# RMSNorm on one core: the first load on 14 DMA engines instead of 16

## The chip, the core and the metric

The kernel runs on one core of a Trainium2 chip. The metric is the device time of one execution in microseconds (us), the median of several runs. A core has five engines with instruction streams of their own: TensorE (PE), VectorE (DVE), ScalarE (ACT), GpSimd (POOL) and SyncE (SP). Sixteen DMA engines move data between HBM, where input and output lie, and SBUF, the memory of 128 partitions in which the engines compute.

## The reference

```python
def reference(x, gamma):            # x: 16 x 1024 x 512 float32, gamma: 512 float32
    eps = 1e-5
    rms = np.sqrt(np.mean(x ** 2, axis=-1, keepdims=True) + eps)
    return (x / rms * gamma).astype(np.float32)
```

Each of the 16,384 rows of 512 numbers is divided by its root mean square and multiplied by gamma. 33.55 MB are read and as much is written.

## The kernel before, in words

The rows are cut into four tiles t = 0 to 3. In a tile each of the 128 partitions holds R = 32 rows that lie one after another in HBM, so a partition's part of a tile is one run of 64 KB. Three SBUF buffers of a whole tile, `slots[0]` to `slots[2]`, hold the tiles; tile 3 uses slot 0 again. A row is overwritten in place by its result.

All DMAs are issued by SyncE, in an order written out by hand. `load(t, slot, r0, r1)` (line 44) brings rows r0 to r1 of all 128 partitions of tile t; `store` (line 48) sends them out. Ahead of any computing SyncE issues, in this order: row 0 of tile 0 ("the first transfer", 256 KB, 2 KB for each partition), rows 1 to 8 ("the second transfer", 14 KB for each partition), gamma in five pieces with the bounds 0, 128, 224, 320, 416, 512 into `gamma_row`, rows 8 to 16, rows 16 to 32, and rows 0 to 16 of tile 1. The scheduler gives DMAs eight semaphores in turn; a DMA whose semaphore was used eight DMAs earlier waits until that one has landed. So the load of rows 16 to 32, the ninth DMA, waits for the first transfer, and the load of tile 1, the tenth, for the second.

TensorE multiplies a row of ones with `gamma_row` (line 66), which puts gamma on all 128 partitions of PSUM (`gamma_psum`); ScalarE copies it to `gamma_b` (line 166) for GpSimd, which works from SBUF.

The rows are then worked on in nine groups (line 76): of 7 and 9 rows of tile 0 first, then of 16 rows. For a group `square_sums` (line 89) squares its rows on ScalarE (line 96) and sums them on VectorE (line 97); `inverse_rms` takes the root on ScalarE (line 102) and the reciprocal on VectorE (line 103). The last rows of a group (`share`, 3 to 7 of them) are scaled and multiplied by gamma on GpSimd (lines 109, 110); the others are scaled on ScalarE, row by row (line 118), and multiplied by gamma on VectorE (line 122). The squares of the group ahead are taken before the scaling of the present one. After each group `transfers` (line 129) issues its stores and further loads:

```python
if (t, g) == (0, 0):
    load(1, 1, 16, 32)
    store(0, 0, 0, 1)
    load(2, 2, 0, 23)
elif (t, g) == (0, 7):
    store(0, 0, 1, 16)
```

The first group needs rows 0 to 7, so the first Square of ScalarE waits for the first two transfers.

Of the kernel before, what the change touches and what calls it, by code (L numbers as in the profile page):

```python
# [9 lines left out]
def kernel(  # L10
# [6 lines left out]
    nc = tc.nc  # L17
    P = nc.NUM_PARTITIONS
# [7 lines left out]
    N, D = xf.shape  # L26
# [3 lines left out]
    xv = xf.rearrange("(t p r) d -> t p r d", p=P, r=R)  # L30
# [9 lines left out]
    slots = [const.tile([P, R, D], fp32, name=f"slot{i}") for i in range(3)]  # L40

    before_scale = []

    def load(t, slot, r0, r1):
        dma = nc.sync.dma_start(out=slots[slot][:, r0:r1], in_=xv[t][:, r0:r1])  # L45
        before_scale.append((slot, r0, r1, dma))

    def store(t, slot, r0, r1):
# [1 line left out]
        before_scale.append((slot, r0, r1, dma))  # L50

    gamma_row = const.tile([1, D], fp32)
    pieces = (0, 128, 224, 320, 416, D)

    load(0, 0, 0, 1)
    load(0, 0, 1, 8)
    for c0, c1 in zip(pieces, pieces[1:]):
        nc.sync.dma_start(out=gamma_row[:, c0:c1], in_=gamma.unsqueeze(0)[:, c0:c1])
    load(0, 0, 8, 16)
    load(0, 0, 16, 32)  # L60
    load(1, 1, 0, 16)
# [105 lines left out]
    for k, group in enumerate(groups):  # L167
        t, g, n, pieces, share = group
# [45 lines left out]
```

## Time and profile before

| | |
|---|---|
| median of 3 runs | 161.56 us (161.54 to 161.67) |
| the profiled execution | 161.71 us, its span 159.9 us |
| busy | DVE 112.0, ACT 107.8, POOL 106.4, PE 2.0 us |
| DMA | 67.12 MB, mean 420 GB/s over the span |
| the first transfer | issued at 0.74 us |
| first Square of ScalarE | starts at 8.33 us |
| last store | issued at 139.2 us |

The span reaches from the first to the last instruction of the program; what the execution counts beyond it lies around the program. A page gives the busy time of each engine, 40 equal slices of the span with the busy share of each engine in tenths, the DMA queues, and the chain of work that ended last. The queue q1 carries the kernel's own transfers, q14 the fetching of instructions. In a row of the timeline there stand the start, the time, the engine (SPq is SyncE's queue), the line, the operation with what it writes and reads, and in brackets how long the engine was idle before and what ended that. A row of the windows has the stretch and its length, the busy times of PE, weight loads, DVE, ACT and POOL with the number of instructions, the clock granted to TensorE, the mean busy share of the 16 DMA engines, and GB/s.

### The profile page before, as it was taken

What the parts mean: (1) busy time and instruction counts of PE and PEld (TensorE: products, weight loads), DVE (VectorE), ACT (ScalarE), POOL (GpSimd) and SP (SyncE); (2) the same over time, 40 slices, a digit from 0 to 9 for tenths busy, and PEclk for the clock granted to TensorE, in tenths of its full rate; (3) what the DMA queues carried; (4) which work ended last, traced back from release to release, by engine and by line L of the source; (5) the groups of instructions that cost most, each with busy time, mean ns of one, the idle gap of its engine ahead of it and who ended that gap; (6) DMA issues with size and microseconds to landing.
All of it is one profiled execution on the core that took longest, in us unless ns stands there. A gap on an engine that the chain in (4) does not pass through costs nothing.

```text
span 159.9 us, 275 instructions
## 1 busy us (share of the span) xinstructions
PE 2.0 (1%) x2; PEld 0.5 (0%) x2; DVE 112.0 (70%) x39; ACT 107.8 (67%) x108; POOL 106.4 (67%) x24
## 2 busy tenths in 40 slices
PE   0050000000000000000000000000000000000000
PEld 0010000000000000000000000000000000000000
DVE  0019098899798999999999999999999009800000
ACT  3071967976999999999889999989960990000000
POOL 1000951994999599999999999999999990000000
DMA  5999999999998999998999999996996996999993
GB/s 182 431 430 467 451 402 434 467 410 393 385 554 389 377 453 407 434 467 381 420 453 443 410 459 451 516 476 286 508 500 279 525 508 279 426 484 402 402 500 148
DMA packets 2603, 67.12 MB, mean 420 GB/s; under 512 B 297, under 2 KB 298, under 8 KB 682
## 3 DMA queue, kind: packets, MB, share of 16 engines
q1 hardware_dynamic: 2602, 67.11, 98.0%
q14 instruction: 1, 0.01, 0.0%
HBM read 33.56 MB, written 33.55 MB: 420 GB/s over the span
## 4 chain that ended last, share of the span: by engine, by line
DVE 59%; ACT 22%; DMA 4%; ACTq 0%; issue 0%; SPq 0%
DVE ss L97 36%; DVE slot L122 23%; ACT slot L118 8%; ACT slot L96 7%; ACT sq_psum L96 6%; DMA slot<-in_x_dram 4%; DVE ss L103 1%; ACT ss L102 1%; ACTq L209 0%; ACT gamma_b L166 0%; SPq L45 0%; ACTq L96 0%
## 5 line engine op out<-in xcount | busy, mean ns | idle before, releaser
L109 POOL TENSOR_TENSOR slot<-slot,ss 128x3584 f32<-128x3584 f32 (+2 forms) x9 | 46.9, 5215 | 24.2 <-DVE ss L103 24.2
L110 POOL TENSOR_TENSOR slot<-slot,gamma_b 128x3584 f32<-128x3584 f32 (+2 forms) x9 | 59.2, 6583 | 0.7
L97 DVE TENSOR_REDUCE ss<-sq_psum 128x7 f32<-128x3584 f32 (+1 forms) x13 | 42.2, 3247 | 13.7 <-ACT sq_psum L96 13.7
L118 ACT ACTIVATE slot<-slot,ss 128x512 f32<-128x512 f32 x75 | 47.2, 707 | 4.7 <-DVE ss L103 4.7
L122 DVE TENSOR_TENSOR slot<-slot,gamma_psum 128x4608 f32<-128x4608 f32 (+2 forms) x9 | 41.3, 4590 | 8.7 <-ACT slot L118 8.7
L96 ACT ACTIVATE sq_psum<-slot 128x3584 f32<-128x3584 f32 (+1 forms) x13 | 34.5, 2656 | 6.3 <-DMA slot<-in_x_dram 5.7
L97 DVE TENSOR_REDUCE ss<-slot 128x9 f32<-128x4608 f32 x3 | 14.9, 4953 | 4.4 <-ACT slot L96 4.2
L97 DVE TENSOR_REDUCE ss<-sq_sbuf 128x5 f32<-128x2560 f32 x5 | 14.0, 2802 | 0.0
L96 ACT ACTIVATE slot<-slot 128x4608 f32<-128x4608 f32 x3 | 12.1, 4032 | 0.0
L96 ACT ACTIVATE sq_sbuf<-slot 128x2560 f32<-128x2560 f32 x5 | 11.6, 2323 | 0.5 <-DMA slot<-in_x_dram 0.5
L102 ACT ACTIVATE ss<-ss,eps_t 128x16 f32<-128x16 f32 (+2 forms) x9 | 2.7, 304 | 11.5 <-DVE ss L97 11.5
L103 DVE RECIPROCAL ss<-ss 128x16 f32<-128x16 f32 (+2 forms) x9 | 2.1, 235 | 0.4 <-ACT ss L102 0.4
L66 PE MATMUL gamma_psum<-gamma_row,ones_col 1*128 1x512 f32 x2 | 2.0, 1122 | 8.8 <-DMA gamma_row<-in_gamma_dram 8.8
L72 ACT ACT_TABLE_LOAD x1 | 1.3, 1283 | 1.2 <-PEq L198 1.2
L166 ACT COPY gamma_b<-gamma_psum 128x512 f32<-128x512 f32 x1 | 0.6, 566 | 0.0
L66 PEld LDWEIGHTS gamma_psum<-gamma_row,ones_col 1*128 1x128 f32 x2 | 0.5, 305 | 8.8 <-issue 8.8
L64 POOL MEMSET ones_col<- 1x128 f32 x1 | 0.2, 194 | 0.3 <-POOLq L198 0.3
L198 POOL MEMSET const-float32-0.0<- 128x1 f32 x1 | 0.1, 99 | 0.2 <-issue 0.2
L72 ACT ACTIVATE table<-eps_t 128x1 f32<-128x1 f32 x1 | 0.2, 203 | 0.0
L198 POOL MEMSET const-bfloat16-1.0<- 128x1 bf16 x1 | 0.1, 102 | 0.0
L198 POOL MEMSET const-uint8-127<- 128x1 uint8 x1 | 0.1, 102 | 0.0
L198 POOL MEMSET const-float32-1.0<- 128x1 f32 x1 | 0.1, 99 | 0.0
(1 smaller groups left out, 0.1 us busy)
## 6 DMA issues: line engine op xcount, KB each, us to landing
slot<-in_x_dram SPq DMA_DIRECT2D x5, 4096.0 KB, 24.3
out_dram<-slot SPq DMA_DIRECT2D x3, 4096.0 KB
out_dram<-slot SPq DMA_DIRECT2D x1, 7936.0 KB
slot<-in_x_dram SPq DMA_DIRECT2D x1, 5888.0 KB
out_dram<-slot SPq DMA_DIRECT2D x1, 3840.0 KB
slot<-in_x_dram SPq DMA_DIRECT2D x1, 2304.0 KB, 25.9
slot<-in_x_dram SPq DMA_DIRECT2D x1, 2048.0 KB, 10.0
slot<-in_x_dram SPq DMA_DIRECT2D x1, 1792.0 KB, 7.1
```

The lines of the kernel that those rows point to most:

```text
L66: nc.tensor.matmul(gamma_psum[:, 0], ones_col, gamma_row, start=True, stop=True)
L72: nc.scalar.activation(out=table, in_=eps_t, func=AF.Sqrt)
L96: nc.scalar.activation(out=sq[:, :m], in_=rows, func=AF.Square)
L97: nc.vector.tensor_reduce(out=ss[:, r : r + m, 0], in_=sq[:, :m], axis=mybir.AxisListType.X, op=OP.add)
L102: nc.scalar.activation(out=ss[:, :n, 0], in_=ss[:, :n, 0], func=AF.Sqrt, bias=eps_t, scale=1.0 / D)
L103: nc.vector.reciprocal(out=ss[:, :n, 0], in_=ss[:, :n, 0])
L109: nc.gpsimd.tensor_tensor(out=part, in0=part, in1=by_row, op=OP.mult)
L110: last = nc.gpsimd.tensor_tensor(out=part, in0=part, in1=gamma_b.to_broadcast([P, share, D]), op=OP.mult)
L118: nc.scalar.activation(out=x[:, g + r, :], in_=x[:, g + r, :], func=AF.Copy, scale=rstd[:, r])
L122: scaled = nc.vector.tensor_tensor(out=part, in0=part, in1=gamma_psum.to_broadcast([P, r1 - r0, D]), op=OP.mult)
L166: nc.scalar.copy(out=gamma_b[:, 0], in_=gamma_psum[:, 0])
L198: nc = _bacc.Bacc("TRN2", target_bir_lowering=False, num_devices=1)
```

## The change

The first transfer takes row 0 of 126 partitions only. Row 0 of the last two partitions follows as a DMA of its own behind the second transfer. Gamma comes in four pieces of 128 numbers where there were five, so that seven DMAs still stand ahead of the load of rows 8 to 16. By the description of the change the first transfer then runs on 14 of the 16 DMA engines. The instructions of the other engines and their order stay as they were.

```diff
-    def load(t, slot, r0, r1):
-        dma = nc.sync.dma_start(out=slots[slot][:, r0:r1], in_=xv[t][:, r0:r1])
+    def load(t, slot, r0, r1, p0=0, p1=P):
+        dma = nc.sync.dma_start(out=slots[slot][p0:p1, r0:r1], in_=xv[t][p0:p1, r0:r1])
         before_scale.append((slot, r0, r1, dma))
...
-    pieces = (0, 128, 224, 320, 416, D)
-
-    load(0, 0, 0, 1)
+    pieces = (0, 128, 256, 384, D)
+    wide = P - 2
+
+    load(0, 0, 0, 1, 0, wide)
     load(0, 0, 1, 8)
+    load(0, 0, 0, 1, wide, P)
     for c0, c1 in zip(pieces, pieces[1:]):
         nc.sync.dma_start(out=gamma_row[:, c0:c1], in_=gamma.unsqueeze(0)[:, c0:c1])
     load(0, 0, 8, 16)
```

## The prediction

> **What bounds the kernel now.** I read the page first: its 40 slices, then the queue table.
>
> ```profile
> span 159.9 us, 275 instructions
> DMA  5999999999998999998999999996996996999993
> q1 hardware_dynamic: 2602, 67.11, 98.0%
> q14 instruction: 1, 0.01, 0.0%
> ```
>
> The 16 DMA engines are busy for 98.0% of the span, while no compute engine passes 70% in the page's first part. A kernel like this ends when its slowest DMA engine has moved its share, so I looked at the DMA by stretches, and at what the DMA queue waits for.
>
> ```profile
> 1.70:3.70 2.00, 0.00 (x0) 0.00 (x0) 0.00 (x0) 0.95 (x2) 0.00 (x0) 1.00 1.05 336
> 3.70:8.30 4.60, 0.00 (x0) 0.00 (x0) 0.00 (x0) 0.00 (x0) 0.00 (x0) 1.00 1.00 419
> 57.00:100.00 43.00, 0.00 (x0) 0.00 (x0) 43.00 (x16) 40.74 (x43) 42.76 (x7) 1.00 1.01 433
> 100.00:140.00 40.00, 0.00 (x0) 0.00 (x0) 31.02 (x11) 26.01 (x33) 31.57 (x6) 1.00 1.00 432
> 140.00:158.00 18.00, 0.00 (x0) 0.00 (x0) 0.00 (x0) 0.00 (x0) 0.00 (x0) 1.00 0.99 426
> ```
>
> The last two figures are the DMA share and GB/s. Share 1.00 in every stretch: the engines are never short of work, even in the last 18 us when nothing computes. The start (336 and 419 GB/s) is poorer than the plateau (432).
>
> ```profile
> 0.74 0.86 SPq L45 DMA_DIRECT2D slot<-in_x_dram  x2
> 1.65 1.48 SPq L58 DMA_DIRECT2D gamma_row<-in_gamma_dram  x5
> 3.17 5.89 SPq L45 DMA_DIRECT2D slot<-in_x_dram  x4
> 8.33 3.16 ACT L96 ACTIVATE sq_psum<-slot 128x3584 f32<-128x3584 f32 x1 [5.67 <-DMA slot<-in_x_dram]
> 8.81 1.19 PE L66 MATMUL gamma_psum<-gamma_row,ones_col 1*128 1x512 f32 x1 [8.81 <-DMA gamma_row<-in_gamma_dram]
> ```
>
> This timeline of the start shows the seven issues that the change touches, and the two instructions that wait for their data.
>
> Last, the trace's single packets. A packet's record has start, duration and size, not its engine; but in steady work a packet starts 4 ns before its engine's previous one ends, so from 7.2 us on the records chain into 16 engines. The last packets of the 16 end between 157.96 and 158.63 us, at a mean of 158.19. Two engines stand apart: one ends at 158.62 ("the last"), one at 158.39; the next are 158.31 and 158.24. The last packet's mark on its semaphore comes at 159.03, SyncE ends its wait at 159.05, the span ends at 159.92, and the execution counts 161.71 us. From the last packet on everything is a fixed tail of 3.09 us, so the time moves one for one with the latest engine. The median of the three runs, 161.56, is 0.15 below this execution; I add differences to the median.
>
> Where the late ones lose time: one engine also carries the instruction packet, 8 KB, from 1.77 to 2.69 us; its first row packet starts at 2.72, against 1.75 to 2.38 on the others. The last engine lost its time in the second transfer: three of its packets there took 0.62, 0.74 and 0.79 us where 0.535 is usual, about 0.54 us in all. In that transfer the 16 engines lost a mean of 0.25 us to such stalls. (Chains in this ramp are less certain.)
>
> **The change part by part.** *First transfer.* 126 rows on 14 engines are nine 2 KB packets each where eight were; such packets follow each other at 80 ns, so 14 engines get +0.08 us. The other two engines lose eight packets, 0.64 us. They can begin the second transfer when its descriptors arrive: it is issued 0.44 us after the first (1.18 and 0.74), and the first one's packets start 1.01 us after their issue, so at about 2.19; that transfer began on the engines at 2.61 to 3.36. So a relieved engine is ahead by 0.4 to 0.9 us, and by 0.64 if it is the one with the instruction packet, where it starts at 2.70.
>
> *The issue of 126 rows.* No row shows one. Bounds: 0.23 us (the shortest one-row issue) and 0.43 us (the longest 128-row one), against 0.38; so -0.15 to +0.05 us on the start of every engine. I take 0, as the row count is nearest to the 128-row issues.
>
> *The two left rows.* 80 ns on each of two engines or 160 ns on one, and about 10 ns for each semaphore packet, behind the second transfer. They land after their engine's second-transfer packets; ScalarE's first Square at 8.33 waits for the last of those (landed 8.24), so it moves by 0 to +0.2 us. That is covered: the first store that needs the result is issued at 27.37, and the engines reach it at about 41.7.
>
> *Gamma.* A 512 B piece with its semaphore packet holds its engine for 29 ns, a 384 B one for 25: five took 0.128 us, four take 0.116, a gain of 0.012 on one engine. That engine ended at 158.23; with two more rows and the gain it ends at 158.38, below 158.62 still.
>
> *SyncE's queue.* Five issues (0.33, 0.23, 0.25, 0.25, 0.25 us) stand between the second transfer and the load of rows 8 to 16; the two-row issue takes the place of one, -0.1 to +0.2 us. Behind it that load is issued at 3.17; the engines reach it at 7.24 at the earliest, so 4 us cover it. The next loads wait for the landings of the first and second transfers (3.72, 8.26) and start on the engines at 12.1 and 21.8. The matmul waits for gamma until 8.81, and its result is first read at 15.65. If the cover at the first load were gone, 0.2 us would go straight to the end. There are still seven DMAs ahead of that load, so the waits of later DMAs on earlier ones keep their places.
>
> *A rule about the small transfer.* The row: the first transfer took from 0.74 to 3.71 to land, 3.0 us for 256 KB, yet five tiny gamma transfers behind the second one landed 0.19 us apart and held their engine for 0.13 us in all. The Trainium skill (DMA: Bandwidth & Descriptors, "Rules for kernel authors") says that under 64 KB a transfer is mostly overhead, and speaks of a fixed cost of about 2 us each. If that were paid in engine time, the new 4 KB transfer would make 163.5; the gamma packets speak against it, the latency lies beside other packets.
>
> *Sum.* If the last engine is one of the two relieved, the end passes to the next: 158.39 + 0.08 = 158.47, -0.15 us; if both late ones are, 158.31 + 0.08 = 158.39, -0.23. Forecast -0.16: 161.40, inside what a measurement of this kernel can tell from no change (0.2%, 0.32 us).
>
> **The rivals.** *The last engine is not one of the two.* It then does nine rows: +0.08 us, 161.64; if the transfer is spread otherwise than the change says, 161.56. For it: the records name no engine, and two of 16 is not many. Against: just two engines stand apart, and lateness from an instruction packet belongs to a fixed place.
>
> *A second hint on place.* The Trainium skill (same page, "Latency and other measured facts") says that engines 7 and 15 are usually slower than the rest, with a guess at a cause. This trace shows equal speed in steady work (1.213 us for 927 of the 1024 packets of 32 KB) and lateness only from the start, so the rule isn't borne out here as a rate; by it, engine 15 relieved would be the forecast, engine 7 late the rival above.
>
> *Slower: a start stall on an engine with nine rows.* The 0.54 us stall of the second transfer falls on another engine, as two engines now read that transfer while 14 still read the first. On an average engine 158.19 + 0.08 + 0.54 = 158.81, +0.19 us, 161.75; on the late one 158.39 + 0.08 + 0.54 = 159.01, +0.39, 161.95. It decides once any engine is over 0.43 us behind the mean. For it: that stretch stalled several engines by 0.1 to 0.5 us. Against: two engines ahead spread the crowd.
>
> *A larger gain.* The start stalls shrink for all. If all engines ended at their mean, 158.19 + 0.08 = 158.27, -0.35 us, 161.21; without the mean stall of 0.25 also, -0.60, 160.96. For it: the start moves 336 and 419 GB/s against 432. Against: 14 of 16 still start together.
>
> **How the numbers follow.** Forecast 0.36, larger gain 0.22, last engine not relieved 0.17, slower 0.25. Range: 161.00 to 161.95, which holds all but the ends of the outer two. Faster by over 0.2% (under 161.24): the larger gain and 0.11 of the forecast, should the first issue be also shorter, 0.33. Slower by over 0.2% (over 161.88): two thirds of the slower rival, 0.17, and 0.04 for a longer first issue with an unrelieved last engine, 0.21. Within: 0.46.
>
> **What would show it.** Right: nine packets of 2 KB on 14 engines, two engines whose first packets are of 14 KB near 2.2 to 2.7 us, last packets ending at 158.4 to 158.5, and a DMA share of 1.00 to the end. Wrong: a last engine at 158.7 or later with a stalled second transfer; a first packet later than 1.75 (the issue); or a DMA share under 0.95 after 57 us, which would mean that the engines wait for compute.

## The result and the profile after

The changed kernel took 162.12 us (median of 18 executions, 161.61 to 163.82) where the kernel before took 161.60 beside it: ratio 1.0049, 95% interval 1.0029 to 1.0070 (close to the ratio of the two means, 1.0048; the two medians alone give 1.0032). That is slower, by more than the 0.2% bound, and outside the range that was given. Of the single times half lie between 161.6 and 162.0, the other half between 162.2 and 163.8, and the median falls in the gap between the two halves. So in this measurement the change costs some 0.2 us in every execution and a half to two more in half of them. The kernel before has such long executions too, but fewer: two of its 18 (162.25 and 163.10 us). The profiled execution of the changed kernel is a long one, 163.11 us with a span of 161.3 (before: 161.71 and 159.9), and shows where these go.

The page and, under it, the DMA by stretches (last two figures: mean busy share of the 16 engines, GB/s):

```profile
span 161.3 us, 274 instructions
...
DMA  5999999999998999999999999899699799699990
...
q1 hardware_dynamic: 2600, 67.11, 97.2%
```

```profile
1.70:3.70 2.00, 0.00 (x0) 0.00 (x0) 0.00 (x0) 0.94 (x2) 0.00 (x0) 1.00 1.05 341
3.70:8.30 4.60, 0.00 (x0) 0.00 (x0) 0.00 (x0) 0.00 (x0) 0.00 (x0) 1.00 1.00 413
140.00:158.00 18.00, 0.00 (x0) 0.00 (x0) 0.00 (x0) 0.00 (x0) 0.00 (x0) 1.00 0.99 430
158.00:160.20 2.20, 0.00 (x0) 0.00 (x0) 0.00 (x0) 0.00 (x0) 0.00 (x0) 1.00 0.04 15
```

Up to 158 us hardly anything is lost: the engines are busy, and 430 GB/s in the last stretch is no less than the 426 before. The loss is a tail. The last of the 40 slices is empty but for little, and from 158.0 to 160.2 the share is 0.04 where the same stretch of before has 0.00:

```profile
158.00:160.20 2.20, 0.00 (x0) 0.00 (x0) 0.00 (x0) 0.00 (x0) 0.00 (x0) 1.00 0.00 0
```

So one engine works alone at the end. (Packets are counted where they start; the last packet starts before 158.9.) Chaining the single packets as in the prediction gives it: 15 engines move their last packet by 158.04 to 158.43 us, the sixteenth by 160.11, 1.67 us later. Before, the last one was 0.24 behind the next.

That engine can be followed back. It is the one that carries the instruction packet, here from 2.32 to 2.69 us. Its rows of the first transfer then take 2.68 to 3.70: nine packets in 1.02 us instead of 0.72, single ones of 0.09 to 0.22 us where 0.084 is usual, at a time when the others already move 14 KB packets. Behind the second transfer, at 8.12, it moves one of the two left rows; the other left row lies on the engine of gamma, at 7.43, just ahead of the four gamma pieces. So one of the two left rows fell on the engine that was already late. The Trainium skill (DMA: Bandwidth & Descriptors, "Why a DMA increments its semaphore by 16 and not by 1") says that a transfer that can't use all 16 engines uses the lowest-numbered ones; that the left row lies on the engine of gamma, whose transfers have one engine, agrees with it. By that rule a short first transfer can only ever relieve the highest-numbered engines; no trace here numbers the engines.

The start in the timeline:

```profile
0.74 1.19 SPq L45 DMA_DIRECT2D slot<-in_x_dram  x3
1.97 1.13 SPq L60 DMA_DIRECT2D gamma_row<-in_gamma_dram  x4
3.14 6.30 SPq L45 DMA_DIRECT2D slot<-in_x_dram  x4
8.96 3.16 ACT L98 ACTIVATE sq_psum<-slot 128x3584 f32<-128x3584 f32 x1 [6.31 <-DMA slot<-in_x_dram]
```

The issues stand as foreseen (the load of rows 8 to 16 at 3.14, before 3.17). The first Square starts at 8.96, 0.63 us later than before, as it waits for the late engine. That isn't what makes the tail: the last store is issued at 140.0 us (139.2 before), and the engines reach it at 148.4 at the earliest.

The late engine then falls back further, in steps. Its lag behind the next one, at the end of each load, in us, worked out from the packets:

| end of load, about | before | changed |
|---|---|---|
| tile 0, rows 8 to 16 (13 us) | 0.14 | 0.46 |
| tile 1, rows 0 to 16 (32 us) | 0.14 | 0.51 |
| tile 1, rows 16 to 32 (42 us) | 0.22 | 0.65 |
| tile 2, rows 0 to 23 (57 us) | 0.20 | 1.14 |
| tile 3, rows 0 to 16 (91 us) | 0.26 | 1.29 |
| tile 3, rows 16 to 32 (101 us) | 0.24 | 1.76 |
| last store (158 us) | 0.24 | 1.67 |

The four jumps, from 42 us on, are the four loads that a store follows. In the last three, the late engine's packets that lost most began at 55.71, 89.33 and 99.81 us (0.39, 0.16 and 0.47 us over the usual), and each was in work while the other 15 turned to stores (56.4 to 56.7, 90.3 to 90.6, 100.6 to 101.0 us). In the loads that end at 91 and 101 us these two packets are the only ones of any engine that took over 0.08 us more than usual; before the change no packet did. In the loads that end at 42 and 57 us packets of all engines lose time, in both kernels. Where another load follows (13 to 32 us, and the short load of tile 2 that ends at 82 us) and in the stores, the lag changes by less than 0.1 us.

### The profile page after: what moved, and what is told of

Same layout as the page of the kernel before. It is cut to its first block, busy times and chain, and to the rows that moved or that the text cites. A ratio compares the mean times of both kernels' runs of the same rounds, so it can differ in the third digit from the quotient of the medians.

```text
span 161.3 us, 274 instructions
## 1 busy us (share of the span) xinstructions
PE 2.0 (1%) x2; PEld 0.5 (0%) x2; DVE 112.1 (70%) x39; ACT 107.8 (67%) x108; POOL 106.4 (66%) x24
## 4 chain that ended last, share of the span: by engine, by line
DVE 36%; ACT 28%; DMA 21%; SPq 1%; ACTq 0%; issue 0%
DMA slot<-in_x_dram 21%; DVE ss L99 19%; DVE slot L124 17%; ACT slot L120 11%; ACT slot L98 7%; ACT sq_psum L98 7%; ACT sq_sbuf L98 1%; ACT ss L104 1%; SPq L45 0%; ACTq L211 0%; DVE ss L105 0%; ACT gamma_b L168 0%; SPq L49 0%; ACTq L98 0%
```

## The experiments

The theory I wanted to test ("L") says two things: the lag of one engine at the start makes the time, and it grows where the others have turned from loads to stores. Rivals: a small transfer behind the second one costs by itself ("N"); rows spread otherwise than eight to an engine make packets collide ("P"). The kernels were timed in three groups, each on one chip and with the kernel before beside it: first the even splits, 8 KB and 16 KB; then 2 KB, the work for all engines alike, the late lag and the run without a first transfer; then 4 KB, the left rows on one engine, 120 partitions and the changed kernel once more. In the three groups 4 of 23, 4 of 35 and 2 of 35 executions of the kernel before took over 162.2 us.

**Even splits.** Rows split so that every engine has eight row packets in all.

```diff
-    wide = P - 2
+    wide = 64
```

> The first transfer takes 64 partitions (four rows on each engine if all 16 are used), the other 64 follow behind the second transfer; gamma in four pieces. The work is even over the engines, as before the change. Theory L (one engine, the one that also carries the instruction packet, is pushed behind the others at the start, and its lag grows whenever the others have turned from loads to stores while it still loads): no engine gets more rows, so the lag at the start of the load of rows 8 to 16 stays at 0.1 to 0.3 us, and the time at 161.5 to 161.8. Theory N (a small row transfer behind the second one costs by itself, by its issue or its place in the queue): slower as the changed kernel, 161.8 to 163.5. Theory P (a spread of rows over the engines other than that of 128 partitions makes small packets collide with the 14 KB packets): some cost, 161.7 to 162.5, if 64 partitions are spread otherwise.

Measured: 162.22 us, ratio 1.0045 (1.0022 to 1.0068). The 161.5 to 161.8 that I had by L was wrong, and the time alone would fit N and P. But the kernel is slower by another way than N's: the trace has no late engine (lag 0.22 us at 13 us, 0.05 at the end). All 16 are late alike: they begin the load of rows 8 to 16 at a mean of 8.05 us instead of 7.51. With four rows fewer ahead of it the second transfer began earlier (14 KB packets from 2.54 us on), but its first packets took 0.53 to 1.55 us, most over 0.88, and most ended at 3.5 to 4.1 us, so the rows moved behind it were added work and nothing was won in front.

```diff
-    wide = P - 2
+    wide = 112
```

> The first transfer takes 112 partitions (seven rows on each of 16 engines), the other 16 partitions follow behind the second transfer, one row on each engine; gamma in four pieces. Even work, but seven rows for each engine, so the rows lie on other partitions of an engine than with 128. Theory L: as before the change, 161.5 to 161.8, lag 0.1 to 0.3 us. Theory P: row packets of 100 to 220 ns in the place of 84 once other engines read 14 KB packets, first large packets of over 0.8 us, and 161.9 to 163.5. Theory N: 161.8 to 163.5.

Measured: 161.52 us, ratio 0.9990 (0.9978 to 1.0003): no cost that shows, and not clearly a gain. So neither the added small transfer (N), nor gamma in four pieces, nor an odd number of rows on an engine (P) costs anything that can be measured here.

The profiled execution is the longest of the 13, 162.36 us, and shows growth where no work was added. One engine, by its chain not the one with the instruction packet, ended the second transfer at 8.18 us, 0.41 after the next; five of its 14 KB packets took 0.63 to 0.81 us. Its lag was 0.36 us at 13 us and 0.55, 0.65, 0.66 and 0.78 at the end of the four loads that a store follows, and it stayed at 0.78 to the end.

**Added lag, 2 to 16 KB on two engines.** The first transfer is whole again; an added load gives more work to the engines of the last two partitions' transfer.

```diff
-    load(0, 0, 0, 1, 0, wide)
+    load(0, 0, 0, 1)
     load(0, 0, 1, 8)
-    load(0, 0, 0, 1, wide, P)
+    nc.sync.dma_start(out=slots[2][wide:P, 0:4], in_=xv[0][wide:P, 0:4])
```

(0:4 is the run with 8 KB; 0:1, 0:2 and 0:8 are those with 2, 4 and 16.)

> The first transfer on all 128 partitions as before the change; behind the second transfer an added load of 2 KB for each of the last two partitions, that nothing needs; gamma in four pieces. It is the changed kernel's two-row transfer alone, without the 126-partition first transfer: 0.08 us on two engines. Theory L (lag of the instruction engine, grown at turns from loads to stores): the added 8 KB cost 1.9 us and 16 KB cost 2.3 us, so 2 KB lie near where growth begins: 161.6 to 162.5, with some runs near 163. Theory N (the lag does not matter, the costs of the 8 and 16 KB loads lay in something else about a two-partition transfer): 163 or more, since the transfer is there as well.

> The first transfer on all 128 partitions as before the change; behind the second transfer an added load of 4 KB for each of the last two partitions, that nothing needs (0.15 us on two engines); gamma in four pieces. In the changed kernel the instruction engine has two 2 KB packets more than before, a ninth row and one of the two left rows (0.17 us). Theory L, amount alone: this run behaves like the changed kernel, a median of 161.8 to 163.2 with runs spread from 161.6 to 163.8. Theory P (it takes the spread of 126 rows over 14 engines as well): as with 2 KB added, 161.5 to 161.9, with few runs above 162.

> The kernel before, with the first transfer on all 128 partitions, and behind the second transfer an added load that nothing needs: 8 KB for each of the last two partitions, into a part of slot 2 that is loaded anew later; gamma in four pieces. It gives two engines 0.30 us of work more and changes nothing else. Theory L: the instruction engine ended the second transfer at 7.62 us in the trace of before and would be at 7.92, as late as the last engine there: lag 0.1 to 0.3, little growth, 161.6 to 161.9. Theories P and N say nothing beyond +0.3 us at most on the end: 161.6 to 161.9.

> As the run with 8 KB, but 16 KB for each of the last two partitions: 0.61 us more on two engines, all else as before the change, gamma in four pieces. The instruction engine would then begin the load of rows 8 to 16 at about 8.23 us, as in the changed kernel (8.21), with no unusual spread. Theory L: its lag grows at the three turns from loads to stores (ends of the loads at about 42, 57 and 101 us) from 0.4 to over 1.2 us, single packets of 32 to 47 KB take 0.2 to 0.5 us more there, and the time is 162.3 to 163.8 in at least some runs. Without growth the end would move from 158.62 to at most 158.99 us, so theories P and N expect 161.6 to 162.0.

| added on each of two engines | work, us | time, us (single times) | ratio to before (95%) |
|---|---|---|---|
| 2 KB | 0.08 | 161.68 (161.49 to 162.31) | 0.9999 (0.9985 to 1.0014) |
| 4 KB | 0.15 | 162.90 (161.70 to 163.58) | 1.0063 (1.0036 to 1.0090) |
| 8 KB | 0.30 | 163.53 (163.35 to 163.76) | 1.0118 (1.0105 to 1.0131) |
| 16 KB | 0.61 | 163.90 (163.63 to 164.04) | 1.0138 (1.0124 to 1.0151) |

This decides for L against N and P: the two-partition transfer of 2 KB, for which N had 163 or more, costs nothing that can be measured, and with 4 KB, for which P had 161.5 to 161.9, the time is 162.90 although the first transfer is whole. Added work of 0.30 us costs 1.9 in the median of its four timed executions (1.7 to 2.1), and doubling it adds only 0.4 more. No theory had the time with 8 KB (161.6 to 161.9 by all three): by L I had taken growth to begin later. The spread of 126 rows isn't needed for the effect.

The amount alone doesn't set the time, though. With 4 KB the instruction engine gets 0.15 us, and nine of 12 times are over 162.2 us; in the changed kernel it gets 0.17, and beside the 4 KB run, on the same chip, only one of 12 was (the last run below). In the changed kernel 12 other engines have a ninth row as well, so its late engine has only one row more than these; no run tests whether that is the reason. The profiled execution with 4 KB is a short one, 161.70 us: there the instruction engine ended the second transfer early, at 7.38 us, and the last engine was 0.07 us behind at 13 us and 0.30 at the end.

The trace with 8 KB shows where. The page, with one row of its DMA issues (KB each, us to landing):

```profile
span 161.6 us, 275 instructions
...
DMA  5999999999989999999999999799799899899990
...
slot<-in_x_dram SPq DMA_DIRECT2D x1, 2304.0 KB, 27.0
```

The same row in the kernel before:

```profile
slot<-in_x_dram SPq DMA_DIRECT2D x1, 2304.0 KB, 25.9
```

The last stretch with 8 KB:

```profile
158.00:160.40 2.40, 0.00 (x0) 0.00 (x0) 0.00 (x0) 0.00 (x0) 0.00 (x0) 1.00 0.07 27
```

The last slice is empty again, the load of 2304 KB lands 27.0 us after its issue (25.9 before), and there is work in a tail: two engines end at 159.96 and 160.32 us, the rest by 158.58. The two were 0.41 us behind the others at 13 us and 1.38 and 1.75 behind at the end of the load of tile 2 (58 us); from there to the end nothing is added. One of them is the instruction engine; the other got nothing added, but had ended the second transfer as the last of all, and its first packet of the load of rows 8 to 16 took 0.98 us where 0.61 is usual. Why that packet was slow isn't shown, so the added load doesn't account for all of this tail by its own work. ScalarE shows the delay, too: among the waits (us in total, times, longest) it waits 1.7 us for a load in this kernel and 0.5 in the one before, shown second (0.7 in the changed one):

```profile
ACT sq_sbuf L98 <- DMA slot<-in_x_dram: 1.7, 1, 1.7
```

```profile
ACT sq_sbuf L96 <- DMA slot<-in_x_dram: 0.5, 1, 0.5
```

Compute isn't late here either: the last store is issued at 140.8 us, and the engines reach it at 148.45 at the earliest.

With 16 KB three engines end 1.68 to 1.89 us behind the rest. In the changed kernel and with 8 and 16 KB the lags come to rest at 1.4 to 1.9 us, but not in every trace: with 112 partitions the lag rests at 0.78.

All the traces but the one of the late lag below can be put side by side. In nine of the 13 the last engine is at most 0.22 us behind at 13 us, and it ends 0.03 to 0.30 behind. In the other four (changed, 112 partitions, 8 KB, 16 KB) one to three engines are 0.36 us or more behind at 13 us, and the last of them ends 0.78 to 1.9 behind the engines that aren't late.

**The same work, for all engines alike.**

```diff
-    nc.sync.dma_start(out=slots[2][wide:P, 0:4], in_=xv[0][wide:P, 0:4])
+    nc.sync.dma_start(out=slots[2][:, 0, 0:256], in_=xv[0][:, 0, 0:256])
```

(Against the run with 8 KB.)

> As the run with 8 KB added on each of two partitions, but the added load takes 1 KB on each of 128 partitions: 8 KB on every one of the 16 engines in eight packets of 1 KB, about 0.4 us for all alike; gamma in four pieces. Theory L: no engine gets further behind the others, so the time rises by the added work alone: 161.8 to 162.3. If added work in that place costs 1.9 us however it is spread: 163.3 to 163.8.

Measured: 162.00 us, ratio 1.0023 (1.0004 to 1.0043): the added work and no more. 8 KB on every engine cost 0.3 us, 8 KB on two engines 1.9.

**The same lag, late in the kernel.**

```diff
-            store(2, 2, 0, 32)
+            store(2, 2, 0, 1, 0, 120)
+            for p in range(120, P, 2):
+                store(2, 2, 0, 1, p, p + 2)
+            store(2, 2, 1, 32)
```

(Against the kernel before; `store` takes the bounds of the partitions here, as `load` does in the changed kernel.)

> The kernel before (first transfer on 128 partitions, gamma in five pieces); late in the kernel the store of tile 2 is cut: row 0 goes out from 120 partitions, then from the last eight partitions in four stores of two partitions, then rows 1 to 32 from all. Two engines get four packets of 2 KB more than the rest (0.32 us), at about 120 us, when no load follows any more. Theory L: a lag that arises behind the last turn from loads to stores doesn't grow: the instruction engine ended at 158.39 and would end at 158.71, so 161.5 to 161.9. If 0.3 us of unevenness costs 1.9 us wherever it lies: 163 to 163.8.

Measured: 162.14 us, ratio 1.0034 (1.0013 to 1.0055). A little over what L gave, and but for one of the 12 times (163.71) far under 163. In the trace the last engine ends 0.32 us behind the next, just what was added, and 0.22 later than in the trace of before (158.85 and 158.63). Most of the rest is SyncE: with the added stores' semaphores it has five waits to go through after the last landing instead of two, 0.19 us more. No growth behind the last load.

**Which part of the change.**

```diff
-    pieces = (0, 128, 256, 384, D)
+    pieces = (0, 128, 320, D)
...
-    load(0, 0, 0, 1, wide, P)
+    for p in (wide, wide + 1):
+        dma = nc.sync.dma_start(
+            out=slots[0][p : p + 1, 0].rearrange("p (a b) -> p a b", a=16),
...
+        before_scale.append((0, 0, 1, dma))
```

> The changed kernel, but the two left rows come as two loads of one partition each behind the second transfer; gamma in three pieces (0, 128, 320, 512), so that seven loads still stand ahead. A load of one partition runs on one engine, as gamma does, so both left rows should fall on the engine of gamma, which was early; the instruction engine keeps the ninth row of the first transfer and loses the left row. Theory L: its extra is 0.08 us, as with the added 2 KB, where the time was 161.68: 161.5 to 162.0 and fewer runs near 163 than the changed kernel. Theory P (the spread of the 126 rows does it): as the changed kernel, 161.8 to 163.2 in the median with half of the runs above 162.

Measured: 161.85 us, ratio 1.0005 (0.9986 to 1.0025), two of 12 times over 162.2. Both rows lie on the engine of gamma in the trace (7.25 and 7.34, gamma at 7.42). The instruction engine, with its ninth row but no left one, begins the load of rows 8 to 16 at 7.52, in the middle of the field; the last engine is 0.07 us behind at 13 us and 0.08 at the end. This fits a left row that takes the instruction engine over the point where its lag grows, but doesn't show it. The instruction packet ended earlier here (2.38 us, and 2.69 in the changed kernel's trace), and the engine began the second transfer at 3.24 and not 3.71, which is more than the 0.08 us of a row. And the executions of the changed kernel itself vary so much (below) that the two can't be told apart by their times alone. The median still stands 0.2 over that of before, within the interval.

```diff
-    wide = P - 2
+    wide = 120
```

> The first transfer takes 120 partitions, if on 15 engines then eight rows on each; the last eight partitions follow behind the second transfer, one row on each of eight engines; gamma in four pieces. One engine is relieved of its first rows, and the instruction engine has one row more than before (0.08 us). Theory L: no growth at that amount, 161.5 to 161.9; and if relief were worth the 0.6 us that the prediction gave it, the relieved engine would end the second transfer among the first (by 7.3 us). By the trace of the changed kernel relief is worth nothing: the relieved engine begins 14 KB packets near 2.5 us, its first ones take 0.8 to 1.2 us, and it ends the second transfer after 7.5 us.

Measured: 161.61 us, ratio 1.0005 (0.9986 to 1.0024). One engine has no row of the first transfer; it begins 14 KB packets at 2.56 us, the first takes 0.90 and the third 0.83, and it ends the second transfer at 7.62 or 7.80 (two chains fit equally well), in both cases after at least 11 of the other 15. Relief bought nothing here either.

**Why relief is worth nothing.**

```diff
-    load(0, 0, 0, 1)
-    load(0, 0, 1, 8)
+    load(0, 0, 0, 8)
```

> The kernel before without the one-row first transfer: rows 0 to 8 come in one load of 128 partitions (packets of 16 KB) issued where the first transfer was; gamma in five pieces. It tests why an engine relieved of its first rows gained nothing: its first 14 KB packets lasted until 3.3 to 3.8 us whenever they began. If large packets at the start are slow to arrive because of their own start (16 engines begin reading large runs at once), the first 16 KB packets end at 3.0 to 3.8 us although nothing precedes them, DMA share in the first 3.7 us falls, and the time is 161.7 to 162.4. If they were slow because small packets of the first transfer were in their way, they begin at 1.75, take about 0.61 us, and the end comes earlier by up to 0.5 us: 161.0 to 161.5.

Measured: 161.62 us, ratio 1.0006 (0.9985 to 1.0028). Nothing stands ahead of these 16 KB packets, and still the first one of 15 engines, begun at 1.75 to 2.37 us, takes 0.73 to 1.45 us where 0.61 is usual, and ends at 2.7 to 3.2. The first large packets are slow without small ones ahead of them; taking small ones away from in front of them doesn't bring them earlier by as much. The time lies between my two expectations, 161.7 to 162.4 for this cause and 161.0 to 161.5 for the other.

**The changed kernel once more.**

> The changed kernel once more, beside the other three on the same chip. Theory L: part of the runs near 161.8, part between 162.2 and 163.8, as the lag of the instruction engine comes out under or over the point where it grows; in the profile, if it is a run near 161.8, the instruction engine begins the load of rows 8 to 16 less than 0.3 us behind the next engine and its lag stays below 0.4 us to the end; if it is a run over 162.5, it begins over 0.3 us behind and its lag grows in the loads ahead of the turns to stores.

Measured: 161.86 us, ratio 1.0015 (0.9992 to 1.0037); one of 12 times is over 162.2, where nine of 18 were in the first measurement. The intervals of the two ratios overlap (1.0029 to 1.0037); how often the long executions come isn't fixed by the kernel alone. Taken by itself this measurement shows no slowdown: its interval holds 1, and 161.86 lies inside the range that was predicted. The profiled one took 161.83 us: the instruction engine begins the load of rows 8 to 16 at 7.76, with others after it, the last engine is 0.07 us behind at 13 us and 0.27 at the end. The instruction packet ended at 2.25 us here (2.69 in the first trace), and though the nine rows behind it were nearly as slow (0.97 us), the engine began the second transfer at 3.23 and not 3.71. The same program, without the start lag, shows little growth. Its page and last stretch:

```profile
span 160.0 us, 274 instructions
...
DMA  5999999999998999998999999996996996999993
```

```profile
158.00:160.40 2.40, 0.00 (x0) 0.00 (x0) 0.00 (x0) 0.00 (x0) 0.00 (x0) 1.00 0.00 0
```

Its last slice is filled (3) and its tail is empty, like those of before.

## Why the prediction was wrong

*The bound* was right: the time is that of the latest DMA engine, and compute is never late. The plateau kept its rate (434 GB/s from 57 to 100 us, 433 before).

*Relief, the first failed term.* The sum had a relieved engine ahead by 0.4 to 0.9 us. In the changed kernel the two relieved engines did begin 14 KB packets at 2.46 and 2.48 us, near the 2.2 to 2.7 that I gave. But their first packets took 1.21 and 0.81 us, later ones up to 0.82, and one of them ended the second transfer at 7.80 or 7.83, among the last three; for the other 7.40 and 7.83 fit equally well. The second trace of the changed kernel is clearer: there one ended at 7.84 and the other, by the chain that fits best, at 7.76, both after 12 of the 14 that had nine rows first. The two latest of before had ended at 7.92 and 7.78. If these are the same engines, which the records don't tell, relief was worth 0.2 us at most in that trace. I subtracted 0.64 us of small packets as if the large ones behind them were ready to run at full speed; the run without a first transfer shows that they aren't.

*Where the added rows fall, the second.* I gave 80 ns to each of two engines and asked only whether the engine of gamma could bear it. It could. The other one was the instruction engine, the second latest of before, and it got the ninth row as well, with nine packets taking 1.02 us for the 0.72 that I had. Even at 0.08 us a row, and one for one, both rows on it make 158.39 + 0.16 = 158.55 and not 158.47.

*"The time moves one for one with the latest engine", the third and largest.* It holds at the very end, but not for a lag at the start: 0.30 us there made 1.9 (8 KB), 0.15 made 1.25 in the median (4 KB). The trace of before hardly shows it, as its last engine was only 0.14 us behind at 13 us and 0.24 at the end; a reader could have seen that its rows prove equal speeds only for engines in step.

*The slower rival* had the side and nearly the place, an engine with nine rows pushed back at the start, and "161.95 on the late one". Its price was only the push; with the growth the same push makes 163. Its chance, 0.25, was low because I held the ramp's stalls for noise.

*The forecast's case* had the end passing to the next engine, and the instruction engine, the second latest of before, did end last in the profiled execution. But it ended at 160.11 us and not at 158.47, and the records don't tell whether the last engine of before was one of the relieved. In the second measurement the median, 161.86, lies in the range; that is no success of the forecast, as the change shows no gain there either.

*The rest.* The issue of 126 rows took 0.45 us, over my upper bound of 0.43; the first packet still started at 1.74 (before 1.75). SyncE's queue and gamma went as worked out. The first Square was later by 0.63 us, not 0 to 0.2, and that was covered as said. The new 4 KB transfer cost no engine its 2 us, which was right against the rule of the Trainium skill that was weighed there (with the added 2 KB, also a transfer of 4 KB in all, the time was 161.68 us); on engines 7 and 15 the runs say nothing more.

*Open.* That growth comes from the others' stores is read from where the lost time lies and from the late-lag run; no run took the stores away, so the mechanism itself (memory, ports) is not shown. Why an engine comes out of the start late in some executions of one program and not in others isn't settled; in the two traces of the changed kernel the end of the instruction packet differs by 0.43 us. So it is open, too, what share of the slowdown is the change's own. Nor is it known why all engines lose time in the loads that end at 42 and 57 us (a mean of 0.44 and 0.13 us in the kernel before).

## What to carry to other kernels

Where all DMA engines are busy all the time, spread each transfer evenly, and look at the packets for the engine that is already late before giving any engine extra work: a few small rows on that one can cost six to eight times their own time (1.25 us for 0.15, 1.9 for 0.30 in this kernel). A lag matters where loads and stores alternate behind it, and hardly where only stores are left. Small packets taken away from in front of large ones are worth their time only if the trace shows that the large ones would run at once.

## What the runs showed of the hardware

- The lag of a DMA engine need not stay what it is: engines at least 0.36 us behind at 13 us fell further behind in loads that a store follows, and the last ended 0.78 to 1.9 behind; where the last one was at most 0.22 behind, it ended 0.03 to 0.30 behind. In time, 0.08 us of added work on two engines gave nothing, 0.30 us gave 1.9 and 0.61 gave 2.3; 0.32 us behind the last load gave 0.5.
- Transfers of two partitions and of one both use the engine that gamma's transfers use; in these traces the second engine of a two-partition transfer is the one that also carries the instruction packet.
- The first large packets after the start take 0.73 to 1.45 us for 16 KB (usual 0.61) even with nothing ahead of them.
